# A planner's duration estimates replaced by durations read from the trace, in a decoder layer on one NeuronCore

## The chip, the cores and the metric

The kernel runs on one core of a Trainium2 chip. The metric is device time in microseconds from start to end of one execution; three runs of the kernel before gave 1162.42, 1163.44 and 1163.62 us, median 1163.44. The engines are TensorE (PE; its weight loads are shown as PEld), VectorE (DVE), ScalarE (ACT), GpSimd (POOL) and SyncE (SP), which issues the transfers.

## The reference

One decoder layer on 16 meta tokens and 256 real tokens, width 2048, float32. It has eight heads of differential attention and eight heads of stick-breaking attention side by side, then an output projection and a squared-ReLU MLP. Cut to what matters:

```python
u = rmsnorm(h, g_mix)
dq, dk, dv, sq, sk, sv = split(u @ w_in)              # six kinds of 1024 columns
dq, dk = rope(rmsnorm(dq, q_g)), rope(rmsnorm(dk, k_g))
# differential heads: softmax(q1 k1) - lam * softmax(q2 k2), causal, applied to dv
o_diff = rmsnorm(diff_attention(dq, dk, dv, lam), diff_out_g) * 0.2
# stick-breaking heads, strictly causal: z = sq.sk * scale
#   log a = log_sigmoid(z) + sum over later keys of log_sigmoid(-z)
o_sb = rmsnorm(stick_breaking_attention(sq, sk, sv), sb_out_g)
h = h + concat(o_diff, o_sb) @ w_out
m = rmsnorm(h, g_mlp)
h = h + square(relu(m @ w_up)) @ w_down               # 8192 hidden columns
```

Meta tokens are dropped from the output.

## The kernel before, in words

**Precision.** Every operand of a large product is split in two parts, `hi` (12 significant bits, a cast on ScalarE, line 164) and `lo` (the rest, a subtraction on VectorE, line 166). A product is then hi x hi + hi x lo + lo x hi. Weights are split as they come in; activations are split when they are made.

**The weight stream.** The weights are read as 96 strips of [128, 16 k-tiles, 256 columns]: strips 0 to 23 belong to the first product (kind by kind, four groups of heads), 24 to 31 to the output product, then four rounds of eight strips up and eight down. A strip has four chunks of four k-tiles. A chunk g goes through three buffers: `raw_g` (512 KB, one transfer by SyncE, five buffers), and `whi_g` and `wlo_g` (three buffers each, `PARTS`), so chunk g + 3 can be split only when TensorE has done with chunk g. The first six chunks are split in two halves of [128, 512]. TensorE multiplies chunk after chunk: two column halves j, four k-tiles each. In the first product one k-tile is three matmuls (lines 815 to 817); from the output product on it is a pair (line 821 with 512 columns, line 820 with 256). The strips that end the first stage and begin the second are interleaved: strips 24 and 25 do chunks 0 to 2 each and then the last chunk by halves, so k-tile 15 of the mixed heads is read last.

**Heads.** Head names are kind, group and number: s31 is stick-breaking, group 3, number 1. A head goes from TensorE to the other engines and back several times: scores (`s0_`, `s1_` or `z_`, line 539), weights on ScalarE and VectorE, transposes of the weights (`pa_`, `pm_`, lines 548 to 557), the weighted values (`po_`, line 579), the sums for the norm (`pn_`, lines 274 and 275), and the split into `mixed`, k-tile 4 * group + 2 * kind + number; s31 gives k-tile 15, d31 k-tile 13.

**What sets the order.** All engines issue in the order in which the program is written down, and that order is made by the class `Pace` when the program is built. It keeps one clock per engine: `pe` is moved by `T` for every group of matmuls, `dve` by `V` and `act` by `A` for every instruction there. `V` and `A` return the time at which a result is taken to be ready. All work beside the weight stream (fetches, weight splits, evacuations, heads) is a job, a Python generator, in one of five lanes; each `yield` names the time at which its next step may be written. After each k-tile of the stream `pump` writes, lane by lane, every step whose time has come on the `pe` clock and whose engine is not more than `QUEUE` (500 ns) behind. `stall` moves the `pe` clock on by 100 ns at a time, letting jobs be written, until the operands of the next k-tile count as ready; no instruction is written for that time. Nothing of this runs on the chip: what is left of it is the order on each engine, and semaphore waits that hold whatever the order is.

Of the kernel before, what the change touches and what calls it, by code (L numbers as in the profile page):

```python
# [36 lines left out]


class Pace:
    """Order of issue: products of the weight stream, with the rest of the work woven in between.  # L40

    Every engine issues in the order of the trace. The jobs (generators) that sit beside the stream yield the time at
    which their next step can run, in estimated nanoseconds of the tensor engine's stream; a step is traced when the
    stream has come that far, so that no engine stands in front of an operand that is not there yet.
    """

    WAIT = 150.0  # from one engine to another
    SLACK = 600.0  # what a result is left to lie before the tensor engine takes it
    QUEUE = 500.0  # how far the other engines may be behind the stream

    def __init__(self, lanes):
        self.pe = self.dve = self.act = 0.0
# [6 lines left out]
        return self.pe + self.WAIT  # L59

    def V(self, n, rate=0.96, after=0.0):
        self.dve = max(self.dve, self.pe, after) + n / rate + 65
        return self.dve + self.WAIT

    def A(self, n, after=0.0):
        self.act = max(self.act, self.pe, after) + n / 1.2 + 93
        return self.act + self.WAIT

    def job(self, lane, gen):
# [5 lines left out]
        yield max(self.at[k] for k in keys), None  # L75

    def take(self, bank, n=1):
        """Wait until n of the banks are free; each is given back with the time of its last use."""
        while sum(t <= self.pe for t in self.banks[bank]) < n:
            yield self.pe + 200, None  # L80
        left = sorted(self.banks[bank])
        self.banks[bank] = left[n:]
# [33 lines left out]
def hymba_layer(ctx: ExitStack, tc: tile.TileContext, xT_d, win_d, wout_d, wup_d, wdn_d, cst_d, par_d, out_d):  # L116
# [10 lines left out]
    pc = Pace((("fetch", 9), ("weights", 9), ("once", 2), ("evac", 6), ("head", 4)))  # L127
# [17 lines left out]
    def retile(tag, shape, name):  # L145
        return rtile(tag, shape, name, SLOTS["e"])

# [1 line left out]
    par = cp.tile([P, G_END], F32, name="par")  # L149
    cst = cp.tile([P, C_END], F32, name="cst")  # L150
    xT = big.tile([P, KT, TOK], F32, name="xT")
# [8 lines left out]
        )  # L160

    def split(hi, lo, src, n):
        """hi + lo == src exactly: hi keeps 12 significant bits, lo the rest."""
        nc.scalar.copy(hi, src)  # L164
        yield pc.A(n), "v"
        nc.vector.tensor_tensor(lo, src, as32(hi), op=ALU.subtract)  # L166
        return pc.V(n)

# [1 line left out]
    strips = []  # L170
    for p, kinds in enumerate(KINDS):
        strips += [("in", kind, p) for kind in kinds]
# [14 lines left out]
    order = list(dict.fromkeys(u[:2] for u in units))  # L187
# [63 lines left out]
        for g in range(RAW + 1, LEAD + RAW):  # L251
            pc.job("fetch", later(g))

# [1 line left out]
    ident = cst[:, C_ID : C_ID + P]  # L255
    cos = cst[:, C_COS : C_COS + TOK]
    sin = cst[:, C_SIN : C_SIN + TOK]
# [12 lines left out]
    Zn = cp.tile([P, 2], F32, name="Zn")  # L270

    def sums(dst, w, hi, lo, n):
        """dst = w.T @ (hi + lo): w is exact in one part."""
        nc.tensor.matmul(dst, lhsT=w, rhs=hi, start=True, stop=False)  # L274
        nc.tensor.matmul(dst, lhsT=w, rhs=lo, start=False, stop=True)  # L275
        return pc.T(2 * n / 2.4 + 6)

    def seed(y, a, v, n, scale, bias=0.0):
        """y near (scale * v + bias) ** -0.5 by tables, and a = y ** 2 * scale / 2 for a Newton step."""
        nc.scalar.activation(y, v, AF.Ln, scale=scale, bias=bias)  # L280
        nc.scalar.activation(y, y, AF.Exp, scale=-0.5)
        nc.scalar.activation(a, y, AF.Square, scale=(0.5 * scale) ** 0.5)
        return pc.A(n, pc.A(n, pc.A(n)))
# [87 lines left out]
        nc.vector.tensor_scalar_mul(Zn, Rn, P**-0.5)  # L371
        pc.at["Rn"] = pc.V(2)

    # Meta keys: the three products of the parts are one, with the parts on rows 0, 32 and 64.
    stack = {n: [cp.tile([P, w], F32R, name=f"stack_{n}{i}") for i in range(2)] for n, w in (("m", SEQ), ("v", P))}
    for t in (*stack["m"], *stack["v"]):
        nc.gpsimd.memset(as32(t[:META_K]), 0.0)

    def split_meta(t, src, n, twice):
        """The parts of src on rows 0, 32 and 64 of t; the row that has the leading part again is twice."""  # L380
        hi, again, lo = t[:META], t[twice : twice + META], t[96 - twice : 96 - twice + META]
        nc.scalar.copy(hi, src)
        t0 = pc.A(n)
        nc.scalar.copy(again, src)
        pc.A(n)
        yield t0, "v"
        nc.vector.tensor_tensor(lo, src, as32(hi), op=ALU.subtract)
        return max(pc.V(n), pc.act + pc.WAIT)

# [1 line left out]
    K, Q, V, RS = {}, {}, {}, {}  # L391

    def rotate(x, g, n, name):
        """x * g * cos and x * g * sin: the rotary embedding, before the 32-row halves of the second change places."""
        a, b = etile("ra", [P, n], f"ra_{name}"), etile("rb", [P, n], f"rb_{name}")
        nc.vector.scalar_tensor_tensor(b, x, g, sin[:, TOK - n :], op0=ALU.mult, op1=ALU.mult)
        tb = pc.V(n + 60)
        nc.vector.scalar_tensor_tensor(a, x, g, cos[:, TOK - n :], op0=ALU.mult, op1=ALU.mult)
        return a, b, tb, pc.V(n + 60)
# [101 lines left out]
        pc.give("acc", pc.at["q", "s", p, j])  # L501

    def values(kind, p, j, o):
        """V of one head with its tokens on partitions, in two parts: real tokens and meta tokens."""
        name = f"{kind}{p}{j}"
        yield from pc.until("R")
        yield pc.pe, "v"
        vt = etile("ra", [P, TOK], f"vt_{name}")
        nc.vector.tensor_tensor(vt, o[:, :TOK], R, op=ALU.mult)
        t = pc.V(TOK)  # L510
        pc.give("acc", t)
        yield t + pc.SLACK, None
        yield from pc.take("att")
        pt = bank("att", f"pv_{name}")
        for b in range(2):
            nc.tensor.transpose(pt[:, P * b : P * b + P], vt[:, META + P * b : META + P * b + P], ident)  # L516
        nc.tensor.transpose(pt[:META, 2 * P : 3 * P], vt[:, :META], ident)
        yield pc.T(330), None
        yield from pc.take("v")
        yield pc.pe, "a"  # L520
        vh = rtile("vh", [P, 2, P], f"vh_{name}", SLOTS["v"])
        vl = rtile("vl", [P, 2, P], f"vl_{name}", SLOTS["v"])
        vm = stack["v"].pop(0)
        ptv = pt[:, : 2 * P].rearrange("p (a b) -> p a b", a=2)
        yield from split(vh, vl, ptv, 2 * P)
        yield pc.pe, "a"
        t = yield from split_meta(vm, pt[:META, 2 * P : 3 * P], P, 32)
        pc.give("att", t)
        V[kind, p, j] = (vh, vl, vm)
        pc.at["v", kind, p, j] = t  # L530

# [1 line left out]
    def scores(parts, q, k, b):  # L533
        """The three products of the parts, for each (destination, rows of the contraction)."""
        n = TOK if b else K0
        cols = slice(P * b, P * b + P)
        for i, (x, y) in enumerate(((0, 0), (0, 1), (1, 0))):
            for dst, rows in parts:
                nc.tensor.matmul(dst, lhsT=q[x][rows, cols], rhs=k[y][rows, :n], start=i == 0, stop=i == 2)  # L539
        return pc.T(3 * len(parts) * max(107, n / 2.4 + 3))  # L540

    def weigh(kind, p, j, a):
        """PO[d, q] = sum over keys of V[key, d] * a[q, key]; a is [128, 272 | 144]."""
        name = f"{kind}{p}{j}"
        yield from pc.take("ah")
        yield from pc.take("att")
# [131 lines left out]
        yield from weigh("s", p, j, t)  # L678

    def head_norm(kind, p, j, po):  # L680
        """Root-mean-square norm over the 128 rows of a head; into mixed."""
        name, n = f"{kind}{p}{j}", SEQ
        i = "ds".index(kind)
        kt, g = 4 * p + 2 * i + j, gout[:, i : i + 1]
# [23 lines left out]
        pc.at["mixed", kt] = yield from split(mixed[:, kt, 0, :], mixed[:, kt, 1, :], a, n)  # L708
        pc.give("n", pc.at["mixed", kt])

# [1 line left out]
    m = hs = R2 = None  # L712

    def residual(f, o):
        """h += the two halves of a product."""
        h = xT[:, f, META:]
        t = etile("rb", [P, SEQ], f"ht_{pc.pe}_{f}")
        nc.vector.tensor_tensor(t, o[:, SEQ:], h, op=ALU.add)
        nc.vector.tensor_tensor(h, o[:, :SEQ], t, op=ALU.add)
        t = pc.V(SEQ, 0.96, pc.V(SEQ))  # L720
        pc.give("acc", t)
        return h, t
# [59 lines left out]
            nc.sync.dma_start(out_d[:, f], h)  # L782
        yield t, None

# [1 line left out]
    def strip_start(s):  # L786
        nonlocal m
        what, a, b = strips[s]
# [17 lines left out]
    def products(s, out, j, k, kk, hi, lo):  # L806
# [4 lines left out]
        if what == "in":  # L811
            f, n = (META, SEQ) if a in (0, 3) else (0, TOK)
            xh, xl = u[:, k, 0, f : f + n], u[:, k, 1, f : f + n]
            o = out[j][:, :n]
            nc.tensor.matmul(o, lhsT=h, rhs=xh, start=first, stop=False)  # L815
            nc.tensor.matmul(o, lhsT=h, rhs=xl, start=False, stop=False)  # L816
            nc.tensor.matmul(o, lhsT=l, rhs=xh, start=False, stop=last)  # L817
            return pc.T(3 * (n / 2.4 + 2.5))
        act = {"out": lambda: mixed, "up": lambda: m, "down": lambda: hid[a]}[what]()
        one = lambda: nc.tensor.matmul(out[j][:, SEQ:], lhsT=l, rhs=act[:, k, 0, :], start=False, stop=False)  # L820
        two = lambda: nc.tensor.matmul(out[j], lhsT=h, rhs=act[:, k, :, :], start=first, stop=last)  # L821
        for f in (one, two) if last else (two, one):
            f()
        return pc.T(768 / 2.4 + 5)

    seen_kinds = set()

# [126 lines left out]
```

## Time and profile before

| | before |
|---|---|
| runs, us | 1162.42, 1163.44, 1163.62 |
| profiled execution, span from first to last instruction, us | 1161.0 |
| PE busy, us and share | 1153.8, 99% |
| PEld busy | 1040.0, 90% |
| DVE busy | 784.5, 68% |
| ACT busy | 660.0, 57% |
| HBM read | 204.39 MB, 178 GB/s over the span |
| mean granted TensorE clock | 1.000 |

The page gives a span for the profiled execution; the median of the runs is 2.4 us longer than that span. How to read the views: a row of groups ends in the busy time of the group, the mean time of one instruction in ns, and the idle time of its engine just before its members with what ended it. A row of the timeline begins with the start in us and the duration in us, and x2 means that two instructions were merged; in square brackets stands the idle time of the engine before it and what ended that. A row of waits has the waiting instruction, what it waited for, and the total in us, the count and the longest. A row of windows has for each engine (PE, PEld, DVE, ACT, POOL) the busy time in that stretch and the instructions, then the granted clock, the share of the transfer engines and GB/s.

### The profile page before, as it was taken

The page shows a single profiled execution, that of the slowest core. Times are in us where ns is not written, and L with a number is a line of the kernel's source. Part 1 is how long each engine was busy: PE and PEld are TensorE (multiplying, and loading weights), DVE is VectorE, ACT ScalarE, POOL GpSimd, SP SyncE. Part 2 cuts the span into 40 slices and gives each one's busy share as a digit, 9 for nine tenths or more (in the row PEclk, how much of TensorE's full clock was granted, in tenths as well). Part 3 has the DMA queues.
Part 4 walks back from the last instruction along what each step waited for, and adds up shares of the span by engine and source line. Part 5 has one row for each costly group of instructions (what it writes and reads, how often), then busy time and mean ns, then how long its engine had stood idle before and what let it go on. Part 6 is the DMA issues. An engine that isn't in the chain of part 4 may idle for free.

```text
span 1161.0 us, 18961 instructions
## 1 busy us (share of the span) xinstructions
PE 1153.8 (99%) x7393; PEld 1040.0 (90%) x7393; DVE 784.5 (68%) x1287; ACT 660.0 (57%) x1131; POOL 1.1 (0%) x8
## 2 busy tenths in 40 slices
PE   8999999999999999999999999999999999999998
PEld 7999999999998888888888888888888888888887
DVE  6998987887877767656555665555566555656654
ACT  7769888779675545554334554334555333555332
POOL 0000000000000000000000000000000000000000
PEclk9999999999999999999999999999999999999999
DMA  8544444444545555555555555555555555555662
GB/s 324 190 144 140 146 146 146 164 158 136 178 136 173 186 192 185 182 189 189 184 184 188 190 182 185 189 189 182 186 192 184 182 188 191 183 183 190 198 219 82
DMA packets 58986, 207.73 MB, mean 179 GB/s; under 512 B 6672, under 2 KB 8848, under 8 KB 58896
## 3 DMA queue, kind: packets, MB, share of 16 engines
q1 hardware_dynamic: 58896, 206.52, 51.5%
q8 instruction: 58, 0.95, 0.3%
q14 instruction: 32, 0.26, 0.1%
HBM read 204.39 MB, written 2.10 MB: 178 GB/s over the span
## 4 chain that ended last, share of the span: by engine, by line
PE 99%; DMA 0%; SPq 0%; DVE 0%; ACT 0%; issue 0%
PE acc L821 47%; PE acc L820 24%; PE acc L815 8%; PE acc L817 8%; PE acc L816 8%; PE s_d L539 1%; PE po_s L579 1%; PE po_d L579 1%; PE z_s L539 0%; DMA raw<-in_win 0%; PE pq_dq L467 0%; PE pv_s L516 0%; PE pv_d L516 0%; SPq L199 0%; PE pn_s L275 0%; PE pn_d L274 0%
## 5 line engine op out<-in xcount | busy, mean ns | idle before, releaser
L166 DVE TENSOR_TENSOR wlo<-raw,whi 128x1024 fp32r<-128x1024 f32 (+1 forms) x390 | 470.2, 1207 | 328.4 <-ACT whi L164 323.7
L164 ACT CAST whi<-raw 128x1024 fp32r<-128x1024 f32 (+1 forms) x390 | 403.5, 1036 | 428.9 <-PE acc L821 399.4
L821 PE MATMUL acc<-hid,whi 128*128 128x512 f32 x1024 | 357.5, 399 | 0.0
L821 PE MATMUL acc<-m,whi 128*128 128x512 f32 x1024 | 357.3, 398 | 0.0
L820 PE MATMUL acc<-hid,wlo 128*128 128x256 f32 x1024 | 277.2, 281 | 0.0
L820 PE MATMUL acc<-m,wlo 128*128 128x256 f32 x1024 | 277.2, 281 | 0.0
L815 PE MATMUL acc<-u,whi 128*128 128x272 f32 (+1 forms) x768 | 223.7, 291 | 2.0 <-ACT whi L164 2.0
L821 PEld LDWEIGHTS acc<-hid,whi 128*128 128x128 f32 x1024 | 188.3, 188 | 41.6
L821 PEld LDWEIGHTS acc<-m,whi 128*128 128x128 f32 x1024 | 188.3, 188 | 41.4
L817 PE MATMUL acc<-u,wlo 128*128 128x272 f32 (+1 forms) x768 | 220.1, 287 | 0.4 <-DVE wlo L166 0.4
L816 PE MATMUL acc<-u,whi 128*128 128x272 f32 (+1 forms) x768 | 219.7, 286 | 0.0
L820 PEld LDWEIGHTS acc<-hid,wlo 128*128 128x128 f32 x1024 | 193.3, 189 | 6.4
L820 PEld LDWEIGHTS acc<-m,wlo 128*128 128x128 f32 x1024 | 193.3, 189 | 6.4
L815 PEld LDWEIGHTS acc<-u,whi 128*128 128x128 f32 x768 | 144.8, 189 | 3.6 <-ACT whi L164 2.7
L817 PEld LDWEIGHTS acc<-u,wlo 128*128 128x128 f32 x768 | 144.7, 188 | 1.0 <-DVE wlo L166 1.0
L816 PEld LDWEIGHTS acc<-u,whi 128*128 128x128 f32 x768 | 145.2, 189 | 0.0
L821 PE MATMUL acc<-mixed,whi 128*128 128x512 f32 x256 | 89.8, 399 | 0.0
L820 PE MATMUL acc<-mixed,wlo 128*128 128x256 f32 x256 | 69.3, 281 | 0.0
L821 PEld LDWEIGHTS acc<-mixed,whi 128*128 128x128 f32 x256 | 47.1, 188 | 10.1
L820 PEld LDWEIGHTS acc<-mixed,wlo 128*128 128x128 f32 x256 | 48.3, 189 | 1.5
L767 ACT COPY ut<-acc 128x256 f32<-128x256 f32 x64 | 23.7, 370 | 15.2 <-PE acc L821 15.2
L773 DVE SCALAR_TENSOR_TENSOR ut<-ut,R 128x256 f32<-128x256 f32 x64 | 27.0, 422 | 1.1
(400 smaller groups left out, 795.2 us busy)
## 6 DMA issues: line engine op xcount, KB each, us to landing
raw<-in_wup SPq DMA_DIRECT2D x128, 512.0 KB, 3.3
raw<-in_wdn SPq DMA_DIRECT2D x128, 512.0 KB, 3.3
raw<-in_win SPq DMA_DIRECT2D x95, 512.0 KB, 3.4
raw<-in_wout SPq DMA_DIRECT2D x32, 512.0 KB, 3.3
out<-xT SPq DMA_DIRECT2D x16, 128.0 KB, 1.7
xT<-in_x SPq DMA_DIRECT2D x3, 544.0 KB, 8.8
cst<-in_cst SPq DMA_DIRECT2D x1, 673.0 KB, 10.3
xT<-in_x SPq DMA_DIRECT2D x2, 272.0 KB, 3.5
```

The costliest lines, as they stand in the source:

```text
L164: nc.scalar.copy(hi, src)
L166: nc.vector.tensor_tensor(lo, src, as32(hi), op=ALU.subtract)
L539: nc.tensor.matmul(dst, lhsT=q[x][rows, cols], rhs=k[y][rows, :n], start=i == 0, stop=i == 2)
L579: nc.tensor.matmul(o, lhsT=l, rhs=r, start=i == 0, stop=i == len(todo) - 1)
L767: nc.scalar.copy(t, o[:, SEQ:])
L773: nc.vector.scalar_tensor_tensor(t, t, 0.0, R2, op0=ALU.max, op1=ALU.mult)
L815: nc.tensor.matmul(o, lhsT=h, rhs=xh, start=first, stop=False)
L816: nc.tensor.matmul(o, lhsT=h, rhs=xl, start=False, stop=False)
L817: nc.tensor.matmul(o, lhsT=l, rhs=xh, start=False, stop=last)
L820: one = lambda: nc.tensor.matmul(out[j][:, SEQ:], lhsT=l, rhs=act[:, k, 0, :], start=False, stop=False)
L821: two = lambda: nc.tensor.matmul(out[j], lhsT=h, rhs=act[:, k, :, :], start=first, stop=last)
```

## The change

The durations that `Pace` adds to its clocks are altered. The fixed part of a VectorE instruction goes from 65 to 140 ns, that of a ScalarE instruction from 93 to 180 ns. A matmul of the stream counts 0.461 ns a column, in place of 1 / 2.4 = 0.417 and a constant of about 2.5 ns; the two matmuls of a norm's sums count at least 112 ns each. The estimates for scores, transposes and weighted values, the transfers, and `WAIT`, `SLACK` and `QUEUE` are left. Comments are emptied.

```diff
     def V(self, n, rate=0.96, after=0.0):
-        self.dve = max(self.dve, self.pe, after) + n / rate + 65
+        self.dve = max(self.dve, self.pe, after) + n / rate + 140
         return self.dve + self.WAIT
 
     def A(self, n, after=0.0):
-        self.act = max(self.act, self.pe, after) + n / 1.2 + 93
+        self.act = max(self.act, self.pe, after) + n / 1.2 + 180
         return self.act + self.WAIT
...
     def sums(dst, w, hi, lo, n):
...
-        return pc.T(2 * n / 2.4 + 6)
+        return pc.T(2 * max(112, 0.461 * n))
...
-            return pc.T(3 * (n / 2.4 + 2.5))
+            return pc.T(3 * 0.461 * n)
...
-        return pc.T(768 / 2.4 + 5)
+        return pc.T(0.461 * 768)
```

The instructions are the same; their order moves. On VectorE at the start, before (`wlo_g` is the low part of chunk g, `u` the split activations of the first product):

```order
L158 SCALAR_TENSOR_TENSOR u_79<-xT_78,par_76,u_79 128x272 x2
L166 TENSOR_TENSOR wlo_0_129<-raw_0_83,whi_0_128 128x512
L158 SCALAR_TENSOR_TENSOR u_79<-xT_78,par_76,u_79 128x272 x2
L166 TENSOR_TENSOR wlo_0_129<-raw_0_83,whi_0_128 128x512
L166 TENSOR_TENSOR wlo_1_131<-raw_1_87,whi_1_130 128x512 x2
L158 SCALAR_TENSOR_TENSOR u_79<-xT_78,par_76,u_79 128x272 x4
L166 TENSOR_TENSOR wlo_2_133<-raw_2_90,whi_2_132 128x512 x2
```

The same engine and place, now:

```order
L158 SCALAR_TENSOR_TENSOR u_79<-xT_78,par_76,u_79 128x272 x4
L166 TENSOR_TENSOR wlo_0_129<-raw_0_83,whi_0_128 128x512 x2
L166 TENSOR_TENSOR wlo_1_131<-raw_1_87,whi_1_130 128x512
L158 SCALAR_TENSOR_TENSOR u_79<-xT_78,par_76,u_79 128x272 x4
L166 TENSOR_TENSOR wlo_1_131<-raw_1_87,whi_1_130 128x512
L166 TENSOR_TENSOR wlo_2_133<-raw_2_90,whi_2_132 128x512
L166 TENSOR_TENSOR wlo_3_194<-raw_3_92,whi_3_193 128x512
```

All four `u` of k-tiles 0 to 3 now stand ahead of the first low part, and the four of k-tiles 4 to 7 between the halves of chunk 1.

On TensorE in strips 24 and 25, before: the norm sums of the last head, `pn_s31`, stand in chunk 99.

```order
L820 MATMUL acc_25_1_5115<-mixed_80,wlo_99_5027 128x256
L274 MATMUL pn_s31_5141<-oh_s31_5109,ones_99 128x256
L275 MATMUL pn_s31_5141<-ol_s31_5110,ones_99 128x256
L821 MATMUL acc_25_1_5115<-mixed_80,whi_99_5026 128x512
L820 MATMUL acc_25_1_5115<-mixed_80,wlo_99_5027 128x256
L821 MATMUL acc_25_0_5114<-mixed_80,whi_100_5070 128x512
L820 MATMUL acc_25_0_5114<-mixed_80,wlo_100_5071 128x256
```

Now, in the second half of chunk 102; the row of line 820 behind the sums is the first to read k-tile 15 of `mixed`:

```order
L579 MATMUL po_s31_5196<-ah_s31_5166,vl_s31_5037 128x128
L821 MATMUL acc_24_0_4882<-mixed_80,whi_102_5043 128x512
L820 MATMUL acc_24_0_4882<-mixed_80,wlo_102_5044 128x256
L274 MATMUL pn_s31_5214<-oh_s31_5210,ones_99 128x256
L275 MATMUL pn_s31_5214<-ol_s31_5211,ones_99 128x256
L820 MATMUL acc_24_0_4882<-mixed_80,wlo_102_5044 128x256
L821 MATMUL acc_24_0_4882<-mixed_80,whi_102_5043 128x512
```

The sums have moved from 26 pairs ahead of the product that reads s31's result to directly in front of it; the transposes `pa_s31`, which stood in chunk 94 of the first product, now stand in chunk 102, behind its first pair.

On ScalarE at that place, now (`z_s31` line 676 is the last Exp of s31's weights, which the transposes read; `po_s31` comes behind them):

```order
L164 CAST whi_104_5140<-raw_104_4946 128x1024
L280 ACTIVATE os_s30_5089<-pn_s30_5126 128x256
L281 ACTIVATE os_s30_5089<-os_s30_5089 128x256
L282 ACTIVATE oa_s30_5150<-os_s30_5089 128x256
L676 ACTIVATE z_s31_5060<-z_s31_5060 128x416
L164 CAST mixed_80<-oa_d31_5131 128x256
L164 CAST ah_s31_5166<-pa_s31_5162 128x384
L382 CAST stack_m1_109<-pm_s31_5168 16x256
L384 CAST stack_m1_109<-pm_s31_5168 16x256
L164 CAST mixed_80<-oa_s30_5150 128x256
L686 ACTIVATE os_s31_5207<-po_s31_5196 128x256
L688 ACTIVATE o_s31_5206<-po_s31_5196,gout_101 128x256
```

The Exp stands behind the casts of chunks 103 and 104 and the norms of d31 and s30.

## The prediction

> **What bounds the kernel now.** I read the page first: busy shares, then the chain that ended last.
>
> ```profile
> span 1161.0 us, 18961 instructions
> PE 1153.8 (99%) x7393; PEld 1040.0 (90%) x7393; DVE 784.5 (68%) x1287; ACT 660.0 (57%) x1131; POOL 1.1 (0%) x8
> PE 99%; DMA 0%; SPq 0%; DVE 0%; ACT 0%; issue 0%
> ```
>
> TensorE is busy for all but 7 us, and the chain is one long walk along TensorE. A busy bar can hide a wait, because matmuls overlap, so the next view is the list of waits on TensorE alone. It has three rows:
>
> ```profile
> PE acc L815 <- ACT whi L164: 2.0, 2, 1.1
> PE warm L860 <- DVE idle L857: 1.2, 1, 1.2
> PE acc L817 <- DVE wlo L166: 0.4, 2, 0.2
> ```
>
> All three lie in the first 10 us (below). After that nothing holds TensorE until its last matmul, so a new order can win at most the 2.0 + 0.4 us of these rows, and every microsecond by which it makes TensorE wait anywhere is a microsecond of the total. The question is only where the new order lets TensorE reach an operand before VectorE or ScalarE has made it. The steady pace, which I need for counting, is a windows row of the MLP:
>
> ```profile
> 700.00:800.00 100.00, 100.00 (x569) 86.72 (x568) 57.71 (x74) 39.27 (x42) 0.00 (x0) 1.00 0.54 187
> ```
>
> 569 matmuls in 100 us are 284.5 pairs (lines 820 and 821), 0.352 us a pair.
>
> **The change part by part.** It alters no instruction's work. Orders differ in three stretches: the first 20 us; the attention steps woven into the first 24 strips; and the hand-over from attention to the output product. From chunk 108 on the orders of VectorE and TensorE are the same but for one row of `hs`, so MLP, last strip and output cost what they cost now: 0.
>
> **Start.** The new VectorE order puts all four pieces of u (k = 0 to 3) ahead of the first low part of the weights, and the next four (k = 4 to 7) between the two halves of chunk 1. The rows of these steps in the trace of before:
>
> ```profile
> 4.69 0.92 DVE L158 SCALAR_TENSOR_TENSOR u<-xT,par,u 128x272 fp32r<-128x272 f32 x2 [3.42 <-ACT u L157]
> 5.68 0.69 DVE L166 TENSOR_TENSOR wlo<-raw,whi 128x512 fp32r<-128x512 f32 x1
> 6.37 0.94 ACT L157 ACTIVATE u<-xT,par 128x272 fp32r<-128x272 f32 x2 [0.73 <-DMA xT<-in_x]
> 6.42 0.19 PEld L817 LDWEIGHTS acc<-u,wlo 128*128 128x128 f32 x1 [0.43 <-DVE wlo L166]
> 6.93 0.91 DVE L158 SCALAR_TENSOR_TENSOR u<-xT,par,u 128x272 fp32r<-128x272 f32 x2 [0.56 <-ACT u L157]
> 8.70 0.69 DVE L166 TENSOR_TENSOR wlo<-raw,whi 128x512 fp32r<-128x512 f32 x1 [0.86 <-ACT whi L164]
> 9.45 0.39 PE L817 MATMUL acc<-u,wlo 128*128 128x256 f32 x1 [0.22 <-DVE wlo L166]
> 9.94 1.29 DVE L166 TENSOR_TENSOR wlo<-raw,whi 128x512 fp32r<-128x512 f32 x2 [0.54 <-ACT whi L164]
> 11.20 1.74 DVE L158 SCALAR_TENSOR_TENSOR u<-xT,par,u 128x272 fp32r<-128x272 f32 x4
> 11.70 0.28 PE L817 MATMUL acc<-u,wlo 128*128 128x256 f32 x1
> ```
>
> VectorE now stands in front of u(2,3), whose high part ScalarE can only start at 6.37 when the activations land. So u(2,3) ends at 6.93 + 0.91 = 7.84, the first low part at 8.53 instead of 6.37, and the first L817 moves from 6.42 to 8.58. Much of that is regained: the second half of chunk 0, which in before waits until 9.45 for its low part (8.70 + 0.69 = 9.39), now finds it ready. The first half has 10 matmuls left at 0.12 us, to 9.8; the second has 12, to 11.3. Chunk 1's first half of low parts still starts at 9.94 and ends near 10.6. Then come the four u: 11.20 + 1.74 = 12.94, bound by ScalarE's u as before, and only then the second half, 0.69 more: 13.63. TensorE needs it at the ninth matmul of chunk 1, in before at 11.70 without a wait, in the new order at about 12.2. It gets it at 13.68. Against before that is 13.68 - 11.70 = **2.0 us**. The chunks behind it I walked the same way to chunk 8: the smallest margin is 0.6 us (second half of chunk 4), so nothing is added, and nothing is regained, because TensorE sets the pace. Bounds: 1.3 if u(4 to 7) and the halves overlap by 0.1 us a step, 2.5 if the restarted matmuls lose 0.1 us each at two or three places.
>
> **Hand-over to the output product.** Here the attention steps of the last head, s31, have slid towards the end: its scores now come with strip 25, and its norm sums (pn_s31) stand directly in front of the product that reads the head's result, mixed tile 15. In before 26 pairs (9.2 us) lie between. Rows of that place in before, and the durations that I use:
>
> ```profile
> 353.98 0.28 PE L275 MATMUL pn_s<-ol_s,ones 128*128 128x256 f32 x1
> 354.10 0.40 PE L821 MATMUL acc<-mixed,whi 128*128 128x512 f32 x1
> 354.36 0.38 ACT L280 ACTIVATE os_s<-pn_s 128x256 f32<-128x256 f32 x1 [1.54 <-PE pn_s L275]
> 355.22 0.42 ACT L282 ACTIVATE oa_s<-os_s 128x256 f32<-128x256 f32 x1
> 359.57 0.42 DVE L166 TENSOR_TENSOR mixed<-oa_s,mixed 128x256 fp32r<-128x256 f32 x1
> 348.05 0.76 PE po_s L579 x7
> L166 DVE TENSOR_TENSOR wlo<-raw,whi 128x1024 fp32r<-128x1024 f32 x378 | 462.5, 1224 | 327.0 <-ACT whi L164 322.3
> L164 ACT CAST whi<-raw 128x1024 fp32r<-128x1024 f32 x378 | 396.7, 1050 | 427.6 <-PE acc L821 399.4 <-PE acc L816 22.8 <-ACT hsq L733 1.8
> L686 ACT ACTIVATE os_s<-po_s 128x256 f32<-128x256 f32 x8 | 3.1, 385 | 1.3 <-PE po_s L579 1.3
> L688 ACT ACTIVATE o_s<-po_s,gout 128x256 f32<-128x256 f32 x8 | 3.8, 472 | 0.0
> L164 ACT CAST oh_s<-os_s 128x256 fp32r<-128x256 f32 x8 | 3.3, 407 | 0.0
> L665 ACT ACTIVATE z_s<-z_s 128x416 f32<-128x416 f32 x8 | 4.4, 546 | 2.0 <-DVE z_s L658 2.0
> L281 ACT ACTIVATE os_s<-os_s 128x256 f32<-128x256 f32 x8 | 3.3, 418 | 0.3
> L672 DVE TENSOR_TENSOR_SCAN cs_s<-cs_s,z_s 128x272 f32<-128x272 f32 x8 | 5.6, 699 | 0.0
> L672 DVE TENSOR_TENSOR_SCAN cs_s<-cs_s,z_s 128x144 f32<-128x144 f32 x8 | 3.6, 454 | 1.8 <-ACT cs_s L668 1.8
> L674 DVE TENSOR_TENSOR z_s<-z_s,cs_s 128x416 f32<-128x416 f32 x8 | 4.7, 593 | 0.3
> L700 DVE TENSOR_TENSOR o_s<-o_s,os_s 128x256 f32<-128x256 f32 x8 | 3.4, 419 | 1.5 <-ACT os_s L281 1.5
> L164 ACT CAST mixed<-oa_s 128x256 fp32r<-128x256 f32 x8 | 3.2, 403 | 0.1
> ```
>
> I count from the end of the seven matmuls po_s30 in the new order. (a) ScalarE has 16 instructions from there to the last Exp of s31's weights: 0.385 + 0.472 + 0.407; four of about 0.55; a weight cast 1.05; Ln, Exp, Square of d31 (0.38 + 0.42 + 0.42); a cast 1.05; the same three of s30; the Exp 0.55: 8.5 us, about 8.2 since independent neighbours overlap a little. TensorE's own stream to the transposes pa_s31, which read that Exp, is 14 pairs and four sums of 0.12 (353.98 to 354.10): 5.4 us. Wait: 2.8. (b) Right behind the five transposes comes the product that reads mixed tile 13 (d31). Its low part is VectorE's eighth instruction behind s31's scans. These can start when ScalarE has done seven of the 16, at 3.4; scans and difference 0.454 + 0.699 + 0.593 make 5.2; two weight low parts and six of 0.42 make 10.2. TensorE, five transposes (0.55) behind the wait, is there at 8.8. Wait: 1.4, so 4.2 together. (c) Seven pairs and po_s31 follow (0.76; its operands are ready), then one pair, and then pn_s31, which needs 0.385 + 0.472 + 0.407 on ScalarE and 0.42 on VectorE: 1.7 less the pair's 0.35. Wait: 1.35. (d) Behind pn_s31 nothing covers the rest. The trace has 353.98 to 355.64 for the sum, Ln, Exp and Square; then two VectorE steps of 0.42, the cast 0.40, the low part 0.42 and four hand-overs of about 0.05: 3.5 less 0.2 of TensorE's own. Wait: 3.3. In before the low part ended at 359.57 + 0.42 = 359.99, 3.2 us before its product at 363.2. Sum 4.2 + 1.35 + 3.3 = 8.9, **9.0** with the slow first matmul after a wait. Bounds: (c) and (d) stand back to back and need no queue, so 4.6 is the floor, with (a) and (b) gone if both engines came early; 12 if they come 3 us late.
>
> **Attention woven into the strips.** Counted at the paces above, the stretches of TensorE work between dependent steps stay, for 15 of 16 heads, at or above 3.8 us (weights to values) and 4.6 (values to norm); only s31 has less (2.6 and 1.2). The tightest place is the scores of head d00, now ahead of strip 4: by the same kind of walk the key's low part is ready 0.2 us before. I take 0, with 3 as upper bound.
>
> **Sum.** 1161.0 + 2.0 + 9.0 = 1172.0 us of span. The runs' median of 1163.44 is 2.4 us above the span, which the change does not touch: **1174.4**.
>
> A rule of the Trainium skill would make it worse. TensorE: Matmul & The Clock Gate, section "Part 1: The HAM clock gate (the "warmup" mystery)", says that an idle window of about 3.4 us halves the clock until some 3.4 us of work have passed. No wait of before is long enough to show it; here two waits of about 3 us would come near.
>
> **The rivals.** (1) *ScalarE and VectorE arrive early*: (a) and (b) vanish, 2.0 + 4.6: 1170.0. For it: both engines are idle a third of the time. Against: their orders are full just there. Chance 0.15. (2) *The clock drops* after the two waits near 3 us. The nine opening matmuls of 512 columns show what a cold array costs, the first ones 0.43 us apart and the last 0.22:
>
> ```profile
> 2.02 0.15 PEld L860 LDWEIGHTS <-idle 128*128 128x128 bf16 x1 [0.28 <-issue]
> 2.45 0.15 PEld L860 LDWEIGHTS <-idle 128*128 128x128 bf16 x1 [0.28 <-issue]
> ```
>
> Six at 0.21 us too much are 1.3 us for a cold start; twice that: 1177.0. The skill's rule above is this mechanism. Chance 0.07. (3) *Waits inside the strips* too, as at d00, 3 us: 1177.4. Chance 0.09. (4) *The hand-over is hidden*: if tile 15 were ready in time only the start counts, 1165.4, within what can be told from no change. It would take 9 us of products behind pn_s31, and there are none. Chance 0.04. (5) *Faster*: the four u together let VectorE run ahead and the start's waits of 2.0 + 0.4 us go, 1161.0. It decides only if activations k = 2, 3 land before VectorE has done u(0,1) at 5.61; the row says 6.37, and the hand-over would have to vanish as well. Chance 0.03.
>
> **How the numbers follow.** The forecast has 0.62; its own range is 1171.5 to 1177.5 (start 1.3 to 2.5, hand-over 7 to 11.5). Rivals 1 to 3 are slower too: slower 0.93, no change 0.04, faster 0.03, where 0.2 per cent (2.3 us) is about what a measurement of this kernel tells from no change. The range of 8 in 10 takes in most of rivals 1 to 3: 1169 to 1179.
>
> **What would show it.** Right: among TensorE's waits a row of L817 behind VectorE of over 2 us near 6 to 9 and one of about 1.4 near 12; and in 345 to 370 us rows of pa_s31 behind ScalarE (2.8), a product behind mixed (1.4 and 3.3) and pn_s31 behind VectorE (1.3); the MLP windows unchanged at 569 matmuls per 100 us. Wrong: no wait at pn_s31 or behind it, which would refute (c) and (d); waits spread over 30 to 340 us, which is rival 3; a granted clock under 1.00 or pairs slower than 0.352 after 360, which is rival 2.

## The result and the profile after

| | us, median (lowest to highest) | against before, 95% interval |
|---|---|---|
| before, all runs | 1163.14 (1162.42 to 1163.62) | |
| the change | 1175.9 (1174.97 to 1176.67) | 1.0111 [1.0097, 1.0126] |

The change makes the kernel 12.8 us slower (11.3 to 14.7 by the interval); 1174.4 was forecast. The page of the changed kernel has the same matmuls, and its chain of waits is again TensorE, now with small parts of VectorE. New is the row of the granted clock, one digit for each 29 us:

```profile
span 1174.9 us, 18969 instructions
PE 1159.8 (99%) x7393; PEld 1044.6 (89%) x7393; DVE 786.4 (67%) x1287; ACT 659.6 (56%) x1131; POOL 1.1 (0%) x8
PE 98%; DVE 1%; ACT 0%; DMA 0%; issue 0%; SPq 0%
PEclk8999999999998999999999999999999999999999
```

The span grew by 13.9 us, the busy time of TensorE by 6.0 with the same 7393 matmuls. So this is not waiting alone: some matmuls took longer. The digit is lowest in the slices 1 and 13, the two places of the prediction. The waits of TensorE (what waited, for what; total in us, times, longest):

```profile
PE acc L820 <- ACT mixed L164: 2.7, 1, 2.7
PE acc L817 <- DVE wlo L166: 2.6, 1, 2.6
PE pa_s L548 <- ACT z_s L676: 2.4, 1, 2.4
...
PE acc L815 <- ACT whi L164: 1.1, 1, 1.1
PE pn_s L274 <- ACT oh_s L164: 0.7, 1, 0.7
PE acc L821 <- DVE mixed L166: 0.6, 1, 0.6
```

All four places named for the hand-over are there, and the one at the start. They sum to 10.1 us without the 1.2 of the opening matmuls (line 860), which is the same in both kernels, against 2.4 before: 7.7 us of the 13.9. The windows of the changed kernel (length; busy time and instructions of PE, PEld, DVE, ACT, POOL; granted clock; share of the transfer engines; GB/s) show the rest:

```profile
0.00:25.00 25.00, 20.09 (x127) 17.54 (x128) 16.18 (x34) 17.96 (x34) 1.06 (x8) 0.86 0.91 338
7.30:14.10 6.80, 5.22 (x24) 5.22 (x25) 5.73 (x11) 4.64 (x10) 0.00 (x0) 0.50 1.01 401
340.00:380.00 40.00, 33.43 (x185) 28.43 (x184) 27.49 (x54) 27.83 (x63) 0.00 (x0) 0.91 0.30 95
365.70:369.00 3.30, 3.30 (x11) 2.76 (x11) 1.33 (x4) 0.54 (x2) 0.00 (x0) 0.51 0.40 140
375.90:379.20 3.30, 3.30 (x12) 2.77 (x12) 2.12 (x5) 1.73 (x4) 0.00 (x0) 0.51 0.00 0
700.00:800.00 100.00, 100.00 (x568) 86.73 (x567) 58.77 (x77) 41.83 (x50) 0.00 (x0) 1.00 0.59 188
```

In three stretches the clock is at half: 6.8 us at the start, and twice some 3.4 us at the hand-over. In the first, 24 matmuls were made where the trace of before has 46; TensorE was idle for 1.6 us of it, in before for 1.1. The MLP is as it was, 568 matmuls in 100 us against 569.

The hand-over row by row on the changed kernel's timeline (start and duration in us; in brackets the idle time before and what ended it):

```profile
363.52 0.53 ACT L676 ACTIVATE z_s<-z_s 128x416 f32<-128x416 f32 x1
364.11 0.33 PE L548 MATMUL pa_s<-cst,z_s 128*128 128x128 f32 x1 [2.39 <-ACT z_s L676]
365.45 0.57 PE L821 MATMUL acc<-mixed,whi 128*128 128x512 f32 x1 [0.58 <-DVE mixed L166]
367.10 0.41 PE L820 MATMUL acc<-mixed,wlo 128*128 128x256 f32 x1
367.74 0.41 PE L820 MATMUL acc<-mixed,wlo 128*128 128x256 f32 x1
371.61 0.38 PE L274 MATMUL pn_s<-oh_s,ones 128*128 128x256 f32 x1 [0.73 <-ACT oh_s L164]
375.18 0.39 PE L820 MATMUL acc<-mixed,wlo 128*128 128x256 f32 x1 [2.72 <-ACT mixed L164]
```

The order of the waits is that of steps (a) to (d): Exp of s31's weights, mixed tile 13, norm sums, mixed tile 15. From the 367.10 to the 367.74 row a pair takes 0.64 us; at full clock it takes 0.352.

### The profile page after: what moved, and what is told of

Its sections match the earlier page's. It is cut to its first block, busy times and chain, and to the rows that moved or that the text cites. A ratio compares the mean times of both kernels' runs of the same rounds, so it can differ in the third digit from the quotient of the medians.

```text
span 1174.9 us, 18969 instructions
## 1 busy us (share of the span) xinstructions
PE 1159.8 (99%) x7393; PEld 1044.6 (89%) x7393; DVE 786.4 (67%) x1287; ACT 659.6 (56%) x1131; POOL 1.1 (0%) x8
## 4 chain that ended last, share of the span: by engine, by line
PE 98%; DVE 1%; ACT 0%; DMA 0%; issue 0%; SPq 0%
PE acc L821 46%; PE acc L820 23%; PE acc L815 8%; PE acc L817 8%; PE acc L816 8%; PE s_d L539 1%; PE po_s L579 1%; PE po_d L579 1%; PE z_s L539 0%; DMA xT<-in_x 0%; PE pq_dq L467 0%; DVE wlo L166 0%; PE pv_s L516 0%; PE pv_d L516 0%; SPq L199 0%
## 5 line engine op out<-in xcount | busy, mean ns | idle before, releaser
L817 PE MATMUL acc<-u,wlo 128*128 128x272 f32 (+1 forms) x768 | 221.0, 288 | 2.6 <-DVE wlo L166 2.6
L817 PEld LDWEIGHTS acc<-u,wlo 128*128 128x128 f32 x768 | 145.9, 190 | 2.9 <-DVE wlo L166 2.9
L821 PE MATMUL acc<-mixed,whi 128*128 128x512 f32 x256 | 92.8, 409 | 0.7 <-DVE mixed L166 0.6
L821 PEld LDWEIGHTS acc<-mixed,whi 128*128 128x128 f32 x256 | 48.4, 194 | 11.1 <-DVE mixed L166 1.1
## 6 DMA issues: line engine op xcount, KB each, us to landing
cst<-in_cst SPq DMA_DIRECT2D x1, 673.0 KB, 10.1
```

## The experiments

Two things stood open. Are the start and the hand-over separate losses, and what makes the order slide? And was the clock's drop really a part of the time, or only something seen beside it? My theory: each of the two places costs what its waits cost, with the half clock on top; the slide comes from the rule that a step is written only when its engine's clock is not more than `QUEUE` (500 ns) behind, a rule whose meaning changes when the engine clocks are made to run longer. The rivals stand in the expectations.

**start_only.** The changed numbers only while the planner's own TensorE clock is under 25 us, the old ones after; the matmul estimates likewise.

```
-        self.dve = ... + n / rate + 65
+        self.dve = ... + n / rate + (140 if self.pe < 25000.0 else 65)
-        self.act = ... + n / 1.2 + 93
+        self.act = ... + n / 1.2 + (180 if self.pe < 25000.0 else 93)
```

> The changed estimates hold only while the planner's TensorE clock is under 25 us; after that the old ones. The order of the first 20 us is that of the change, the last head's norm sums stand 9.4 us of products ahead of the product that reads it, as before. Theory (two separate costs: a start of about 3.1 us, made of a longer wait and a stretch at half clock, and a hand-over of about 10.8 us): 1163.1 + 3.1 = 1166.2 us, one wait of L817 of about 2.6 us and a granted clock of 0.5 for about 7 us behind it. Rival (a late start is made up where the attention steps have room, as TensorE then finds its operands earlier): 1163.1 us. Rival as in the prediction (the start costs 2.0 us by waits alone, clock full): 1165.1 us.

Measured: 1165.65 us, ratio 1.0026 [1.0015, 1.0038], 3.0 us more than the 1162.63 of before on that chip. Its waits of TensorE and its window at the hand-over:

```profile
PE acc L817 <- DVE wlo L166: 2.9, 1, 2.9
...
340.00:380.00 40.00, 40.00 (x248) 35.64 (x247) 30.54 (x55) 26.38 (x51) 0.00 (x0) 1.00 0.52 162
```

The start's wait is there, and the hand-over is full again, with 40.00 us of 40 busy. The matmuls of the start ran at half clock here too. The window of the start doesn't show it, since it reads 1.00, against the 0.5 that I had expected there; the spacing of the matmuls does. Here are that window and two matmuls of 256 columns, one in the half rate, whose successor starts 0.21 us later at 12.97, and one behind it, whose successor starts 0.12 us later at 13.85:

```profile
0.00:25.00 25.00, 20.01 (x125) 16.88 (x125) 15.87 (x33) 17.86 (x34) 1.05 (x8) 1.00 0.90 329
...
12.76 0.41 PE L815 MATMUL acc<-u,whi 128*128 128x256 f32 x1
13.73 0.28 PE L817 MATMUL acc<-u,wlo 128*128 128x256 f32 x1
```

So a granted clock of 1.00 near the start of a profile can hide a half rate. In this execution all nine opening matmuls are some 0.42 us apart, from 1.19 to 4.58, so the clock may never have been up before 13.5, rather than have fallen.

**handover_only.** The same split, the other way round: old numbers below 25 us, changed ones after.

```
+        self.dve = ... + n / rate + (65 if self.pe < 25000.0 else 140)
+        self.act = ... + n / 1.2 + (93 if self.pe < 25000.0 else 180)
```

> The reverse: old estimates while the planner's TensorE clock is under 25 us, the changed ones after that. The first 20 us are as before; the last head's norm sums stand directly ahead of the product that reads it. Theory of two separate costs: 1163.1 + 10.8 = 1173.9 less what the profile of the changed kernel counts twice, so 1172.5 to 1174 us, with waits of TensorE of about 2.4, 0.6, 0.7 and 2.7 us between 350 and 380 us. Rival (the start moved the heads, the estimates after it do not matter): 1163 to 1164 us.

Measured: 1173.73 us, ratio 1.0096 [1.0079, 1.0113], 11.1 us more. Its waits are those of the whole change at the hand-over, with those of before at the start:

```profile
PE acc L820 <- ACT mixed L164: 2.7, 1, 2.7
PE pa_s L548 <- ACT z_s L676: 2.4, 1, 2.4
...
PE acc L817 <- DVE wlo L166: 0.5, 2, 0.2
```

The two halves add to 14.1 us, against the 12.8 of the change, within their intervals (1.7 to 4.4, and 9.2 to 13.1). So the losses are separate. Its profiled execution took 1172.1 us, 1.6 below the median of its runs, and had only one stretch at half clock at the hand-over where the changed kernel's has two: the waits are the same in these two profiled executions, the half-clock stretches are not. The mean granted clock on record for each of its four executions goes the same way: 0.998, 0.997, 0.996 and 0.995 for 1172.10, 1173.61, 1173.85 and 1173.99 us.

**queue_2000.** The changed numbers, with a wider gate.

```
-    QUEUE = 500.0
+    QUEUE = 2000.0
```

> The changed kernel with QUEUE at 2000 in place of 500 ns: a step may be written while its engine's clock is up to 2 us ahead of TensorE's. Durations as in the change. In the order the last head's scores come 34 us earlier and its norm sums 10.8 us of products ahead of the product that reads it; the first 20 us are as in the change. Theory (the gate of 500 ns, not the durations, pushes the heads back once the engines' clocks run truer and so mostly stand above it): the hand-over costs nothing, the start stays: 1166.2 us. Rival (the later ready times themselves do it): order aside, waits stay and the time is 1174 to 1176 us.

Measured: 1166.82 us, ratio 1.0035 [1.0022, 1.0048], 4.2 us more than before and 9.1 less than the change. The hand-over's waits are gone, the start's stays. The head of its list has the 2.1 us of the start and 0.4 at 206 us; another wait of 0.3 stands at 63 us:

```profile
PE acc L817 <- DVE wlo L166: 2.5, 2, 2.1
```

This settles what makes the steps of s31 slide: the gate, since the durations are those of the change and only the gate is wider. How the slide builds up is argued: with the longer durations VectorE and ScalarE count as more than 500 ns behind more often (how often was not counted), attention steps are written later than before, and after 16 heads the last one has no products left to stand behind. With the wider gate there are 10.8 us of products between s31's norm sums and the product that reads its result, counted in the order at 0.352 us a pair; in the change there are none. Of the 4.2 us that remain, 1.7 stand at the 25th group of the stream (a group is the three matmuls of one k-tile, and the 25th opens the fourth chunk; 18.16 against 16.45 us in the traces) and about 1.8 inside the strips, which no term of mine had.

**fill_waits.** The whole change, and 40 matmuls of 512 columns on the idle warm-up tile, whose result nobody reads, written where TensorE waits: 11 ahead of the first L817, 11 ahead of pa_s31, 4 ahead of pn_s31 and 14 behind its sums. The order of all else is that of the change.

```
+    fill = lambda dst, times: [nc.tensor.matmul(dst, lhsT=idle[:, :P], rhs=idle, start=True, stop=True) for _ in range(times)]
...
+        fill(p1, 11 * (name == "s31"))
+        fill(pn, 4 * (name == "s31"))
+        fill(bank("att", "fill"), 14)
+        s == 0 and k == 0 and j == 0 and fill(warm, 11)
```

> The changed kernel with 40 added matmuls of zeros (128x512, bf16, into spare PSUM banks, read by nobody) in TensorE's order where it waits: 11 ahead of the first L817, 11 ahead of pa_s31, 4 ahead of pn_s31, 14 behind it. At 0.22 us each they fit into the waits of 2.6, 2.4, 0.9 and 3.0 us. Nothing else moves. Theory (the clock dropped because TensorE was idle, and the half clock costs 1.5 us at the start, where a wait for the second half of chunk 1 comes in its place, and about 3.2 at the hand-over): granted clock 1.00 throughout, 1171.2 us. Rival (the half clock costs nothing, since the other engines' chain sets the time there): 1175.9 us or a little more.

Measured: 1172.26 us, ratio 1.0083 [1.0068, 1.0098], 3.6 us less than the change with 40 matmuls more. The clock is full at both places, and the waits that the filling leaves are small. Windows and waits of this kernel, and the row where the second half of chunk 1 starts:

```profile
0.00:25.00 25.00, 22.44 (x151) 18.15 (x152) 16.81 (x34) 18.98 (x35) 1.06 (x8) 1.00 0.92 347
340.00:380.00 40.00, 39.20 (x229) 31.20 (x230) 30.29 (x57) 29.48 (x65) 0.00 (x0) 1.00 0.34 107
...
PE acc L821 <- DVE mixed L166: 0.6, 1, 0.6
...
13.17 0.39 PE L817 MATMUL acc<-u,wlo 128*128 128x256 f32 x1 [0.92 <-DVE wlo L166]
```

So the half clock is a part of the time, not a thing beside it. Between the profiled executions the gain is 4.5 us (spans 1174.9 and 1170.4), near the 4.7 expected; between the medians it is 3.6. The changed kernel's profiled execution was its slowest, 1176.67, and has the lowest mean clock of its four, 0.994; the others have 0.997, 0.997 and 0.995 for 1175.92, 1175.88 and 1174.97 us. So fewer half-clock stretches there are a likely cause of the difference, though time and clock don't go in step as in handover_only. The four executions of fill_waits all have 1.00 and lie within 0.7 us.

**tensor_only.** The changed matmul estimates alone; VectorE and ScalarE back at 65 and 93.

```
-        return pc.T(2 * n / 2.4 + 6)
+        return pc.T(2 * max(112, 0.461 * n))
```

> Only the TensorE numbers are changed (0.461 ns a column, at least 112 ns a sum); VectorE and ScalarE keep 65 and 93 ns. In the order the start is that of before and the last head's norm sums stand 9.4 us of products ahead of the product that reads it. Theory (the fixed parts of VectorE and ScalarE push the heads back, the TensorE numbers do not): 1162.6 us, no wait of TensorE behind the first 10 us. Rival (any change of one clock against the others does it): 1165 us or more.

Measured: 1167.15 us, ratio 1.0041 [1.0028, 1.0055], 4.3 us more than the 1162.82 of before on that chip. I had 1162.6; the theory falls here, and the rival holds. The start and the hand-over are as in before; the loss lies inside the strips, in front of attention matmuls. The largest wait is

```profile
PE po_s L579 <- DVE stack_m L387: 0.6, 1, 0.6
```

Only 1.6 us of the loss show as idle time (TensorE is busy for 313.42 of the 315 us from 25 to 340); the rest, it seems, lies in gaps that the recorded durations of the matmuls cover. A TensorE clock that runs faster in the plan (more ns a matmul) makes a result seem to be old enough after fewer matmuls, so that attention steps are written earlier in the stream, and here too early: the weights' stacks are not there yet. That reading of the order is argued, the sign is measured, and so is the place of the waits.

**vector_only** and **scalar_only.** Each of the other two numbers alone, in the kernel before: 140 for 65 on VectorE, or 180 for 93 on ScalarE.

```
# vector_only
+        self.dve = max(self.dve, self.pe, after) + n / rate + 140
# scalar_only
+        self.act = max(self.act, self.pe, after) + n / 1.2 + 180
```

> Only the fixed part of VectorE is changed (140 ns). In the order the last head's scores end 7.3 us of products ahead of the product that reads its result (11.6 in the changed kernel, 47 in before), and the norm sums 0.6 us ahead of it. Theory (each fixed part alone is enough, since a step goes only when its engine's clock is inside the gate): hand-over at least that of the changed kernel, 1174 to 1179 us. Rival (it takes both): under 1170 us.

> Only the fixed part of ScalarE is changed (180 ns). In the order the start is nearly that of the change (four u ahead of the first low part), and the last head's scores end 6.5 us of products ahead of the product that reads its result, the norm sums 0.1 us ahead of it. Theory (each fixed part alone is enough): start 3 us and hand-over 10 to 15 us, 1175 to 1180 us. Rival (it takes both): under 1170 us.

Measured: 1185.69 us, ratio 1.0197 [1.0183, 1.0211], and 1182.66 us, ratio 1.017 [1.0156, 1.0184]: 22.9 and 19.8 us more than before, each worse than all three changes together, and more than I expected by 7 and 3 us at the nearer end. Two rows of the waits of each, vector_only first:

```profile
PE pa_s L548 <- ACT z_s L676: 5.8, 1, 5.8
PE pn_s L274 <- ACT oh_s L164: 2.0, 1, 2.0
```

```profile
PE po_s L579 <- DVE stack_m L387: 3.9, 2, 2.6
PE acc L820 <- ACT mixed L164: 2.7, 1, 2.7
```

These are waits of the hand-over again (they stand between 364 and 381 us), and longer in sum, since s31 has slid further. The clock adds to them: from 340 to 380 us it is granted at 0.87 and 0.88 in the mean, in the changed kernel at 0.91. In scalar_only 2.4 us of the loss lie at the start (25th group at 18.81). The table has TensorE's own work, in us, that the order puts between two steps of s31:

| kernel | scores of s31 to its transposes | norm sums to the product of tile 15 | us against before |
|---|---|---|---|
| before | 18.5 | 9.2 | |
| the change | 7.0 | 0.1 | +12.8 |
| queue_2000 | 16.7 | 10.8 | +4.2 |
| tensor_only | 16.1 | 9.4 | +4.3 |
| vector_only | 2.2 | 0.6 | +22.9 |
| scalar_only | 4.2 | 0.1 | +19.8 |

My reading is that the measure of one clock against another decides: a longer VectorE or ScalarE clock alone closes the gate most, and a longer matmul beside it takes part of that back, since all three clocks then run faster together. The times and the table agree with it; the gate itself was not watched.

Are the new numbers truer, as the expectation for queue_2000 has it? As durations of one instruction they are. But the planner adds them up, and what one instruction adds to a row of independent ones is the time from start to start. A low part of 512 columns lasts 0.69 us and two in a row 1.29 (the rows at 5.68 and 9.94 under the prediction), so the second starts 0.60 us behind the first: 512 / 0.96 = 533 ns and 67 more, where the old number is 65 and the new one 140. ScalarE's casts of 512 columns in before:

```profile
5.02 0.62 ACT L164 CAST whi<-raw 128x512 fp32r<-128x512 f32 x1
9.29 1.14 ACT L164 CAST whi<-raw 128x512 fp32r<-128x512 f32 x2 [0.61 <-DMA raw<-in_win]
```

The second starts 1.14 - 0.62 = 0.52 us behind the first: 512 / 1.2 = 427 ns and 93 more, which is the old number; the new one is 180. So for independent neighbours the new engine clocks run ahead of the engines, by some 75 to 87 ns an instruction, and some six of them use up the gate of 500 ns. Only the matmul's 0.461 ns a column is the measured pace (0.352 us for 768 columns).

**both_undone.** Could the change be made harmless? Old numbers below 25 us, changed ones after, and the wide gate throughout.

```
-    QUEUE = 500.0
+    QUEUE = 2000.0
...
+        self.dve = ... + n / rate + (65 if self.pe < 25000.0 else 140)
```

> The changed estimates from 25 us of the planner's clock on, the old ones before that, and QUEUE at 2000 ns. The start is that of before; norm sums of the last head 7.3 us of products ahead of the product that reads it. Theory (start and hand-over are all that the change costs): 1162.6 to 1163.5 us, no row of TensorE waiting between 10 us and the end. Rival (part of the loss lies inside the strips, where TensorE's stream is now cut by attention steps 100 times in place of 89): 1164 to 1165 us.

Measured: 1166.52 us, ratio 1.0035 [1.0023, 1.0046], 3.7 us more than before, above both expectations. Neither the start's nor the hand-over's loss is there; new waits stand at 31, 121 and 207 us, where the order has steps of the heads' rotary embedding on VectorE in front of a weight split that TensorE needs:

```profile
PE acc L817 <- DVE wlo L166: 1.6, 3, 0.7
```

No version tried is faster than before. The waits of before leave 2.4 us to win, and each of these orders gives back more than that somewhere.

## Why the prediction was right, and where its steps were not

**Direction and time: right.** TensorE had no slack behind the first 10 us, so each wait that an order adds is in the time. 1175.9 lies 1.5 us from the forecast and inside its own range. But two errors of size and one missing term partly cancel. At full clock the changed kernel would have come near the 1172.3 of fill_waits, 2.1 below the forecast, so that 1175.9 lies so near is in part luck.

**Start (2.0).** Measured 3.2 us in the traces (25th group of the stream at 19.64 against 16.45 us), 3.0 with start_only. The first wait came as walked: low part ready and L817 off at 8.88, where 8.58 was forecast (ScalarE could start at 6.75, when the activations landed, and not at 6.37). The second, at the second half of chunk 1, did not come. The half-clock stretch made TensorE reach that half only at 14.88, when its low part, the first of the two in the row of 12.65, was ready near 13.3, as these rows of the changed kernel show:

```profile
8.14 1.96 DVE L166 TENSOR_TENSOR wlo<-raw,whi 128x512 fp32r<-128x512 f32 x3
8.88 0.58 PE L817 MATMUL acc<-u,wlo 128*128 128x256 f32 x1 [2.64 <-DVE wlo L166]
9.26 0.42 PE L815 MATMUL acc<-u,whi 128*128 128x256 f32 x1
12.65 1.28 DVE L166 TENSOR_TENSOR wlo<-raw,whi 128x512 fp32r<-128x512 f32 x2
14.88 0.28 PE L817 MATMUL acc<-u,wlo 128*128 128x256 f32 x1
```

With the clock held up by the filling, the second wait appears, 0.92 us at 13.17, and the 25th group starts at 18.02: 1.6 us by waits alone, for the 2.0 forecast. So the step was sound and somewhat long, and the clock took its place with 1.6 us more; some 0.2 of these are no matter of the clock, since the activations of k = 4 to 7 were there at 10.22 in fill_waits and at 10.44 in the changed kernel.

**Hand-over (9.0).** The four waits stand where they were put, (a) and (b) behind whom they were put. At pn_s31 the row names ScalarE's cast, where the list of signs had VectorE; VectorE's low part came 0.3 us later still, before the second matmul of the sums. At (d) it names ScalarE's cast too, since line 820 reads the high part. Their sizes, by the rows of waits: (a) 2.4 for 2.8; (b) 0.6 for 1.4; (c) 0.7 for 1.35; (d) 2.7 for 3.3. The rows leave out the slow matmuls at each stop. By the gaps between the starts of matmuls the four are 2.6, 0.7, 1.2 and 3.3, 7.9 us with two more 0.1 to 0.2 long. So (a) and (d) were right and (b) and (c) too large, by 0.9 us together. The cause is the duration that I took for a row of instructions on one engine. Three ScalarE instructions of the changed kernel:

```profile
356.28 0.38 ACT L686 ACTIVATE os_s<-po_s 128x256 f32<-128x256 f32 x1
356.56 0.47 ACT L688 ACTIVATE o_s<-po_s,gout 128x256 f32<-128x256 f32 x1
356.92 0.41 ACT L164 CAST oh_s<-os_s 128x256 fp32r<-128x256 f32 x1
```

They last 0.38 and 0.47 and start 0.28 and 0.36 us apart: independent neighbours overlap by 0.1 us each. I added the full durations along (b), where eight such instructions stand in a row on VectorE, and (c), where there are four, and took off 0.3 only in (a).

**The clock (rival 2, 0.07).** It did drop, beside the waits of the forecast and not in their place, and the sign that I had named for it is there: a granted clock under 1.00 and pairs slower than 0.352 us after 360. My chance for it was too small. Its price of 2.6 us was less than the 4.5 that fill_waits gained between the profiled executions. Each stretch of 3.4 us at half clock does 1.9 us of full-speed work (3.4 x 0.352 / 0.64), a loss of 1.5; two of them at the hand-over are 3.1, and 1.6 at the start make 4.7. The Trainium skill, TensorE: Matmul & The Clock Gate, "Part 1: The HAM clock gate (the "warmup" mystery)", says that the clock goes to half after at least one idle window of about 3.4 us, for some 3.4 us of work. The trace agrees with the half rate and with stretches that are one window long (3.4 us) or two (6.8). Of the longer one the first half was not full of work: TensorE waited until 8.88. The trace does not agree with the idle window. Stretches of some 3.3 us of TensorE that stand ahead of the three drops, in the changed kernel:

```profile
3.90:7.20 3.30, 1.26 (x6) 0.40 (x3) 0.91 (x2) 1.99 (x5) 0.00 (x0) 1.00 0.97 309
362.30:365.60 3.30, 0.92 (x6) 0.61 (x7) 3.30 (x8) 2.86 (x9) 0.00 (x0) 1.00 0.66 179
372.60:375.80 3.20, 0.55 (x2) 0.35 (x3) 1.70 (x4) 1.51 (x4) 0.00 (x0) 1.00 0.00 0
```

and two that no half clock followed, the first in the changed kernel, the second the start of before:

```profile
369.10:372.40 3.30, 2.49 (x15) 1.78 (x13) 0.43 (x1) 1.04 (x3) 0.00 (x0) 0.99 0.00 0
```

```profile
3.90:7.20 3.30, 1.98 (x12) 1.18 (x10) 1.88 (x4) 2.33 (x5) 0.00 (x0) 1.00 0.92 298
```

TensorE was busy for 38, 28 and 17 per cent of the stretches that cost the clock, and for 75 and 60 of those that didn't. No wait of the changed kernel reached 3.4 us; the longest idle time is 2.7. I had read the rule as one that needs a wait of that length, and gave it 0.07 for that reason.

**Strips (0).** None of the waits in the list stands there, so as waits the step was right. Attention groups interrupt the stream of products 102 times up to the end of the hand-over, 89 times in before, which costs little. Behind most groups the second product starts some 0.2 us after the first, in place of 0.12; but behind transposes, such as this group of before, the first starts early, 0.02 to 0.03 us after the last of them, where transposes are 0.11 apart:

```profile
331.38 0.27 PE L557 MATMUL pm_s<-cst,z_s 128*16 128x128 f32 x1
331.40 0.37 PE L815 MATMUL acc<-u,whi 128*128 128x272 f32 x1
331.62 0.29 PE L816 MATMUL acc<-u,whi 128*128 128x272 f32 x1
```

Counted over both products, and up to the hand-over, the groups cost 3.1 us in before and 3.4 in the changed kernel: 0.3 us that I left out. **MLP and output (0)**: right within 0.2 us.

**The sum.** In the profiled executions 3.2 at the start, 7.9 of waits and 3.1 of half clock at the hand-over and 0.3 of the interruptions make 14.5, where 13.9 was measured. fill_waits gives the parts without counting them: at full clock it is 1.6 us behind before at the 25th group and 9.4 at the end (spans 1170.4 and 1161.0), so strips and hand-over cost 7.8 by waits, for the 9.0 forecast. The changed kernel loses 13.9 - 3.2 = 10.7 there, of which 2.9 are then the half clock. By the medians the forecast of 11.0 over before was 1.8 too low: waits 1.5 too high in sum, the clock left out.

**The other rivals.** (1), engines early, falls: (a) and (b) are there at 3.3 us together by starts. (3), waits inside the strips, falls for this kernel, though not for tensor_only, queue_2000 and both_undone. (4) and (5) fall.

## What to carry to other kernels

An order made by a planner with its own clocks depends on how these clocks stand to each other and to the gates that were set with them; putting recorded durations in for one of the numbers, or for all of them, isn't an improvement while the gates stay as they are, and here the new VectorE or ScalarE number alone cost more than all of them. A clock that adds up one engine's instructions wants the time from start to start; the recorded duration holds an overlap that it then counts twice. On a kernel whose bounding engine never waits, walk each engine's new order to the first place where an operand comes late, with start-to-start times of neighbours and not their durations. Then ask what a wait of 2 to 3 us does to the clock behind it: here that added about half of what the waits themselves cost.

## What was not expected of the hardware

The clock of the changed kernel fell to half after waits of 2.4 to 2.7 us, when TensorE had been busy for 17 to 38 per cent of some 3.3 us; at 60 and 75 per cent it stayed. The first drop lasted 6.8 us, with 1.6 of them still in the wait, the later ones 3.4. Forty extra matmuls in the waits made the kernel 3.6 us faster than the change without them. Near the start the granted clock of a profile can read 1.00 while matmuls run at half rate (start_only), so the spacing of matmuls is the safer sign. And two independent neighbours on VectorE or ScalarE start some 0.1 us sooner than the duration of the first says.
